# Partial sums of a down projection: kept in SBUF and added to DRAM at the end, with a larger descriptor store

## The chip, the cores and the metric

The kernel runs on one core of a Trainium2 chip. The metric is device time in microseconds (us), the median of several runs; one further run was profiled, and all rows of a trace come from that one. The engines of the core are named as in the profile: PE (matrix multiply), PEld (its weight loads), DVE (vector), ACT (activations and copies), POOL (general, and the one that issues DMAs through descriptors that it writes itself into a store in SBUF) and SP (issues most DMAs). Every engine works through its own queue in order and waits on semaphores of the others.

## The reference, cut to what matters

The reference is one inference step of a small encoder with two layers. Nine tiles of 128 tokens (1024 prompt tokens and 128 sample tokens) by 1024 features run through, in each layer, an attention with its output projection, and then a squared-ReLU MLP:

```python
def mlp(x, g_norm, w_up, w_down):
    return jnp.square(jax.nn.relu(rmsnorm(x, g_norm) @ w_up)) @ w_down
...
        hp = hp + ap @ w_o_a[i]
...
        hp = hp + mlp(hp, g_mlp[layer], w_up[layer], w_down[layer])
        hs = hs + mlp(hs, g_mlp[layer], w_up[layer], w_down[layer])
```

w_up is 1024 x 4096, w_down 4096 x 1024, everything is float32. The change touches the MLP and, a little, the output projection ahead of it.

## The kernel before, in words

**Number format.** Each float32 operand of a matmul is split into a high part (ACT, a cast) and the rest (DVE, a subtraction), helper `split`, lines 125 to 134. A product is three matmuls: high by high, high by low, low by high (`mm3`, lines 744 to 748).

**Stages.** A layer is attention (`attention`), output projection (`wo_phase`), up stage (`mlp_up`) and down stage (`mlp_down`), layer after layer (`run`, lines 1280 to 1301). The running sum x of the nine tiles lives in DRAM as `xp`, three parts of three tiles (`PARTS`: part 0 is tiles 5, 6, 7; part 1 is 2, 3, 4; part 2 is the sample tile, 0 and 1); `xd[t]` is tile t of it.

**Up stage** (lines 778 to 908). 16 blocks of 256 columns of w_up; products of sums of blocks, Strassen-like, in the PSUM tiles X, Y and Z. In each block `sample` multiplies the sample tile into `ps_s8`; ACT applies ReLU and square into an SBUF tile `h8` (128 x 256); `turn` (lines 838 to 843) transposes its two halves on PE (L841) and ACT copies them to the first 128 columns of the two h tiles `eh` (L843). The last three products of a block go to Y, X and Y; between the two in Y, DVE evicts Y (L878, `tt(v[3], Y, v[3])`). The h tiles and sums of them go to DRAM in 20 forms (`hd`), by POOL DMAs (L911).

**Down stage** (lines 968 to 1157). 40 steps (20 products for each half of the 4096 rows), in an order written out as `CHAINS`. A step n takes one form of h (`a`, 128 x 1536, loaded from `hd` by SP, L1026, split by ACT and DVE) and one sum of blocks of w_down (`r`, loaded by SP, L1026; sum `s` by DVE, L1062; split into `w`), and does 36 matmuls of 128 x 512 into three PSUM banks `ps_c`, one bank for each of three token tiles. Steps of one chain add up in the same banks; six banks allow two sets. `reads` of a step tells to which halves of which parts of x the banks are added after it. There are two ways:

- The part's x tiles are in SBUF already: DVE adds the bank to the tile (L1141).
- They are not: ACT copies the bank to one of two tiles `o` (L1138), and POOL adds the tile of three banks to `xp` in DRAM by an accumulating DMA of 768 KB (L1148). The two `o` tiles are used in turn, by steps 0, 1, 2, 3, 4, 8, 9, 10, 11, 12, 14, 28, 31 and 32.

`X_AT = {1: 2, 12: 1, 32: 0}` says that part 2 is loaded to SBUF after step 1, part 1 after step 12 and part 0 after step 32, each as three POOL DMAs from `xd` (`load_x`, L1084) that must wait for the accumulates into the same rows. After the last step that reads a part (30 for part 2, 35 for part 1, 39 for part 0) SP stores its three tiles (L1145): to `xd` in layer 0, to the output in layer 1.

**What sets the order.** A planner of the framework lays out each engine's queue from priorities and a simulation. The kernel adds orders by hand: `behind(a, b)` puts b after a on their engine, `follow` keeps PE's products, `chain` DVE's instructions of the down stage and `load` SP's loads in the order of the program. The loads of the first three steps and the splits of step 0 (`low[0]`: first that of `a`, then that of `w`) are emitted before the loop over the steps and have a raised priority, so that they run beside the last up block. `late` is a list of form sums of the last up blocks that DVE does in the first down steps. In layer 0, `prep_bias` (lines 1164 to 1194) and the next layer's first weight loads and splits (POOL L185, DVE L190) run beside the down stage.

**Memory.** POOL's DMAs take their descriptors from a store whose size is `dynamic_dma_scratch_size` (line 1849), 1024 bytes in each partition. The tiles of the down stage are laid out by `DOWN_HOME` over those of the up stage; a pad of 504 floats behind the bias tiles keeps the places of the rest.

**Output projection** (lines 643 to 735). `load_o` loads the attention's output of a tile from DRAM; in layer 1 it has two halves to be added, the second of which is loaded to a tile `o2`, and DVE adds them.

Of the kernel before, what the change touches and what calls it, by code (L numbers as in the profile page):

```python
# [8 lines left out]
F32 = mybir.dt.float32  # L9
F32R = mybir.dt.float32r  # L10
AF = mybir.ActivationFunctionType
ALU = mybir.AluOpType
# [4 lines left out]
P = 128  # L17
# [10 lines left out]
FB = 256  # L28
# [66 lines left out]
class Build:  # L95
# [547 lines left out]
    def wo_phase(self, layer, sx, x8, wo):  # L643
        nc = self.nc
        with ExitStack() as st:
            self.psum_pools(st, f"wo{layer}", dict(m=(4, 1), g=(3, 1)), dict(m="m", n="g"))
            work = self.pool(st, f"wow{layer}")
            small = self.pool(st, f"wosm{layer}", 2)
            osp, xs = {}, {}
            lo, hi = slice(0, 512), slice(512, 1024)  # L650

            def O(t, z):
                if t in self.kept:
                    xs[t] = self.kept[t]
                    return
                if len(xs) % 5 < 2:
                    xs[t] = self.rawp.tile([P, D], F32, tag="raw", name="x")
                else:
                    xs[t] = work.tile([P, D], F32, tag="x", name="x", bufs=3)
                nc.sync.dma_start(xs[t], self.xd[t])  # L660
                if t in self.wo_done:
                    return
                with self.tc.high_priority(WO_PRIO) if len(osp) < 2 else nullcontext():
                    load_o(t, z)

            def second():
                self.last = work.tile([P, 4, P], F32, tag="o2", name="o2")
                return self.last

            def load_o(t, z):  # L670
                o = work.tile([P, 4, P], F32, tag=f"o{z}", name="o")
                self.load_halves(layer, 1, t, o, second, nc.vector)
                oh = work.tile([P, 4, P], F32R, tag=f"oh{z}", name="oh")
                ol = work.tile([P, 4, P], F32R, tag=f"ol{z}", name="ol")
                self.split(oh, ol, o)
                osp[t] = oh, ol

            def M(t):
                x = xs[t]
                for n in range(2) if t not in self.wo_done else ():  # L680
# [36 lines left out]
            for n, t in enumerate(order):  # L717
                if n + 2 < NTILE:
                    O(order[n + 2], z % 2)
                    z += order[n + 2] not in self.wo_done  # L720
                M(t)
                ready.add(t)
                for f in pend:
                    f()
                pend = []
                if t == ST:
                    def sample():
                        for h in range(2):
# [49 lines left out]
    def mlp_up(self, layer, sx, x8, rp, raw0):  # L778
        nc = self.nc
        tt = nc.vector.tensor_tensor  # L780
        with ExitStack() as st:
# [36 lines left out]
            def act(t, src):  # L818
                a = nc.scalar.activation(t, src, AF.Relu)
                nc.scalar.activation(t, t, AF.Square)  # L820
                return a

            def sample(quad):
                s8 = self.psum("s", [P, FB], "ps_s8")
                z = []
                for h in range(2):
                    for k in range(4):
                        kk = h * 4 + k
                        z.append(self.mm3(
                            s8, x8[0][:, kk], x8[1][:, kk], quad[h][0][:, k], quad[h][1][:, k],  # L830
                            kk == 0, kk == KC - 1,
                        ))
                self.follow(z[0][0], z[-1][1])
                h8 = hp.tile([P, FB], F32, tag="h8", name="h8")
                self.marks = [act(h8, s8)]
                return h8

            def turn(eh, h8):
                t8 = self.psum("t", [P, 2, P], "ps_t8")
                for h in range(2):  # L840
                    nc.tensor.transpose(t8[:, h], h8[:, h * P : h * P + P], self.ident)  # L841
                for h in range(2):
                    nc.scalar.copy(eh[h][:, 0:P], t8[:, h])  # L843

            def tokens(eh, quad, ws, c, with_sample):
# [25 lines left out]
                product(X, 5, False, True)  # L871
                nc.scalar.copy(v[1], X)
                if with_sample:
                    h8 = sample(quad)
                product(X, 6, False, True)
                a = nc.scalar.copy(v[3], X)
                product(Y, 4, True, True)
# [4 lines left out]
                product(X, 3, False, True)  # L882
                act(v[2], X)
                if with_sample:
                    turn(eh, h8)
                product(Y, 2, False, True)
                tt(v[1], Y, v[1], ALU.add)
                act(v[1], v[1])
# [79 lines left out]
    def mlp_down(self, layer, out):  # L968
# [3 lines left out]
        with ExitStack() as st:  # L972
# [15 lines left out]
            for n, tags in enumerate(DOWN_HOME):  # L988
                pool = self.pool(st, f"d{n}_{layer}")
                for t in tags.split():  # L990
                    if t == "bias":
                        self.bias_tiles(pool)
                        pool.tile([P, 504], F32, tag="pad", name="pad")
                    elif t[0] == "+":
                        pool.tile([P, int(t[1:])], F32, tag="gap", name="gap")
                    else:
                        homes[t] = pool
                        slots[t] = fresh(t)
# [79 lines left out]
            def early(n):  # L1078
                return self.tc.high_priority(EARLY[n]) if n < len(EARLY) else nullcontext()

            def load_x(i):
                for t in PARTS[i]:
                    xs[t] = take(f"x{t}")
                    nc.gpsimd.dma_start(xs[t], self.xd[t])  # L1084

            for n in range(AHEAD):
                with early(n):
# [8 lines left out]
            def chain(z):  # L1096
# [2 lines left out]
                self.dve = z  # L1099
                return z  # L1100

            for z in (*low[0], total_of.get(1)):
                if z is not None:
                    chain(z)
            late = iter(self.late)
            for n, (s, p, g, first, final, reads, _) in enumerate(seq):
# [17 lines left out]
                for i in range(3):  # L1124
# [11 lines left out]
                    for o, v in reads:  # L1136
                        if o in adds:
                            nc.scalar.activation(adds[o][:, i], banks[i], AF.Copy, scale=float(v))  # L1138
                            continue
                        x = xs[PARTS[o // 2][i]][:, N[o % 2]]  # L1140
                        chain(tt(x, x, banks[i], ALU.add if v > 0 else ALU.subtract))  # L1141
                    for part in {o // 2 for o, _ in reads}:
                        if last[part] == n:
                            t = PARTS[part][i]
                            nc.sync.dma_start(out(t), xs[t])  # L1145
                for o, z in adds.items():
                    dst = self.xp[o // 2][:, :, N[o % 2]].rearrange("t p n -> p t n")
                    nc.gpsimd.dma_start(dst, z, accum_op=ALU.add)  # L1148
                if n in X_AT:
                    load_x(X_AT[n])  # L1150
                for _, z in zip(range(LATER), late):
                    chain(z)
                for m in range(n + 1, total):
# [657 lines left out]
TAIL = 6  # L1811
LATER = 3
AHEAD = 3
X_AT = {1: 2, 12: 1, 32: 0}
WO_ORDER = [[0, 4, 1, 5, 2, 6, 7, 3, ST], [0, 4, 1, 5, 6, 2, 7, 3, ST]]

CFG = [
# [49 lines left out]
```

## Time and profile before

| | us |
|---|---|
| median of 3 runs | 2400.55 (2395.85 to 2406.25) |
| profiled run, its own time | 2405.0 |
| its span, first to last instruction | 2403.2 |
| PE busy in the span | 2285.3 |
| DVE busy | 1735.2 |
| ACT busy | 1317.3 |
| POOL busy | 632.8 |

A row of a timeline gives the start in us, the duration in us, the engine, the line, the operation, what it writes and reads, the shape and the count; in brackets stands how long the engine had been idle before it, and what ended that. A row of the groups gives the count, then busy us and the mean of one in ns, then the idle time before the group's instructions and what ended most of it. A row of the waits gives the waiting engine and line, for what it waited, the total in us, how often, and the longest. A row of the windows gives busy time and, in parentheses, the count of each engine, then the granted PE clock, the busy share of the DMA engines and GB/s. A busy PE is not PE at its peak: its matmuls overlap, and 36 of 128 x 512 follow each other at a spacing well below the duration of one.

### The profile page before, as it was taken

How to read it: one execution, taken by the hardware profiler on the slowest of the kernel's cores; microseconds unless marked ns; L12 is line 12 of the kernel's file. 1: busy time of each engine (PE TensorE's matmuls, PEld its weight loads, DVE VectorE, ACT ScalarE, POOL GpSimd, SP SyncE). 2: the span in 40 equal slices, each digit the busy share in tenths (PEclk: the TensorE clock that was granted, in tenths of full speed). 3: DMA queues.
4: the chain of work that ended last, by engine and by line, in shares of the span. 5: the costliest groups of instructions: out<-in, count | busy, mean ns of one | idle time of the engine just before them, and what ended most of it. 6: DMA issues, size and time to landing. Idle time of an engine off the chain costs nothing.

```text
span 2403.2 us, 33331 instructions
## 1 busy us (share of the span) xinstructions
PE 2285.3 (95%) x11429; PEld 1904.2 (79%) x11429; DVE 1735.2 (72%) x3108; ACT 1317.3 (55%) x2587; POOL 632.8 (26%) x938
## 2 busy tenths in 40 slices
PE   7998999899999978999999999998999999889999
PEld 6787877788888767887777788886888888678887
DVE  6788786666566567998677876877665664678986
ACT  3777674555555534444367666665655555444452
POOL 4333332222222111002333434354122222111000
PEclk9999999999999989999999999999999999999999
DMA  7335546234343789657554655555243444878554
GB/s 251 120 111 166 170 149 200 88 131 147 125 139 124 222 241 228 209 145 232 190 153 113 194 154 176 166 171 168 86 147 122 143 147 138 255 169 227 193 155 148
DMA packets 227577, 397.41 MB, mean 165 GB/s; under 512 B 51592, under 2 KB 126288, under 8 KB 227408
## 3 DMA queue, kind: packets, MB, share of 16 engines
q1 hardware_dynamic: 190544, 291.45, 38.2%
q0 software_dynamic: 35568, 99.11, 14.5%
q10 hardware_dynamic: 1296, 4.72, 0.5%
q8 instruction: 90, 1.47, 0.3%
q14 instruction: 79, 0.65, 0.1%
HBM read 241.23 MB, written 152.92 MB: 164 GB/s over the span
## 4 chain that ended last, share of the span: by engine, by line
PE 76%; DVE 8%; DMA 7%; issue 4%; ACT 3%; POOL 1%; SPq 0%; ACTq 0%; POOLq 0%; DVEq 0%
PE ps_c L746 7%; PE ps_c L747 7%; PE ps_c L748 7%; PE ps_x L746 5%; PE ps_x L748 5%; PE ps_x L747 5%; PE ps_mm L217 4%; PE ps_mm L219 3%; PE ps_mm L218 3%; PE ps_y L746 2%; PE ps_y L748 2%; PE ps_y L747 2%; DMA a<-hd 2%; PE ps_tr L324 2%; PE ps_mm L176 1%
## 5 line engine op out<-in xcount | busy, mean ns | idle before, releaser
L746 PE MATMUL ps_c<-w,a 128*128 128x512 f32 x960 | 377.5, 393 | 36.0 <-ACT o L1138 27.8
L747 PE MATMUL ps_c<-w,a 128*128 128x512 f32 x960 | 376.3, 392 | 3.0 <-DVE w L134 3.0
L748 PE MATMUL ps_c<-w,a 128*128 128x512 f32 x960 | 375.7, 391 | 0.0
L911 POOL DMA_DIRECT2D hd<-h x272 | 149.0, 548 | 608.2 <-ACT h L820 368.8
L746 PEld LDWEIGHTS ps_c<-w,a 128*128 128x128 f32 x960 | 182.1, 190 | 76.2 <-ACT o L1138 29.0
L747 PEld LDWEIGHTS ps_c<-w,a 128*128 128x128 f32 x960 | 182.2, 190 | 41.8 <-DVE w L134 3.7
L748 PEld LDWEIGHTS ps_c<-w,a 128*128 128x128 f32 x960 | 181.8, 189 | 38.1
L128 ACT CAST a<-a 128x1536 fp32r<-128x1536 f32 x80 | 118.7, 1484 | 158.7 <-DMA a<-hd 158.7
L134 DVE TENSOR_TENSOR a<-a 128x1536 fp32r<-128x1536 f32 x80 | 140.3, 1753 | 78.0 <-ACT a L128 77.8
L217 PE MATMUL ps_mm<-w,hh 128*128 128x512 f32 x432 | 173.9, 404 | 7.6 <-POOL w L185 2.6
L219 PE MATMUL ps_mm<-w,hl 128*128 128x512 f32 x432 | 172.7, 401 | 1.0 <-DMA hl<-hTd 0.8
L218 PE MATMUL ps_mm<-w,hh 128*128 128x512 f32 x432 | 171.8, 399 | 1.3 <-DVE w L190 1.1
L746 PE MATMUL ps_x<-sx,w 128*128 128x512 f32 (+1 forms) x408 | 158.3, 388 | 3.9 <-ACT h L867 2.7
L128 ACT CAST w<-s 128x2048 fp32r<-128x2048 f32 x56 | 107.0, 1912 | 95.7 <-DVE s L1062 90.8
L1148 POOL DMA_DIRECT2D xp<-o x28 | 36.3, 1297 | 464.2 <-ACT o L1138 364.6
L128 ACT CAST w<-ru 128x512 fp32r<-128x512 f32 (+1 forms) x160 | 110.0, 708 | 84.1 <-PE ps_y L747 32.0
L748 PE MATMUL ps_x<-sx,w 128*128 128x512 f32 (+1 forms) x408 | 154.7, 379 | 0.0
L747 PE MATMUL ps_x<-sx,w 128*128 128x512 f32 (+1 forms) x408 | 154.7, 379 | 0.0
L134 DVE TENSOR_TENSOR w<-s,w 128x2048 fp32r<-128x2048 f32 x56 | 128.2, 2289 | 30.7 <-ACT w L128 30.7
L134 DVE TENSOR_TENSOR ptl<-ps_tr,pth 128x512 fp32r<-128x512 f32 x180 | 122.3, 685 | 24.3 <-ACT pth L128 19.2
L134 DVE TENSOR_TENSOR w<-ru,w 128x512 fp32r<-128x512 f32 (+1 forms) x160 | 126.7, 794 | 14.9 <-ACT w L128 14.8
L128 ACT CAST pth<-ps_tr 128x512 fp32r<-128x512 f32 x180 | 105.0, 595 | 45.7 <-PE ps_tr L324 37.2
(269 smaller groups left out, 6098.2 us busy)
## 6 DMA issues: line engine op xcount, KB each, us to landing
a<-hd SPq DMA_DIRECT2D x80, 768.0 KB, 4.8
hd<-h POOLq DMA_DIRECT2D x272, 192.0 KB, 2.5
ru<-in_w_up SPq DMA_DIRECT2D x64, 512.0 KB, 3.8
r<-in_w_down SPq DMA_DIRECT2D x32, 1024.0 KB, 9.4
xp<-o POOLq DMA_DIRECT2D x28, 768.0 KB, 7.7
o<-oTd SPq DMA_DIRECT2D x52, 256.0 KB, 4.5
x<-xp SPq DMA_DIRECT2D x23, 512.0 KB, 4.9
xp<-xo SPq DMA_DIRECT2D x18, 512.0 KB, 2.8
```

Source lines behind the costliest of these rows:

```text
L128: a = nc.scalar.copy(hi, src)
L134: return a, e.tensor_tensor(lo, src, hi.bitcast(F32), ALU.subtract)
L176: nc.tensor.matmul(ps, oh[:, k, :], w[:, 0, k, nn], start=(k == 0), stop=False)
L217: nc.tensor.matmul(ps, a, w[:, 0, k, :], start=(k == 0), stop=False)
L218: nc.tensor.matmul(ps, a, w[:, 1, k, :], start=False, stop=False)
L219: self.lp = nc.tensor.matmul(ps, b, w[:, 0, k, :], start=False, stop=(k == KC - 1))
L324: self.lp = nc.tensor.transpose(pt[:, i, :], get(i), self.ident)
L746: a = mm(ps, ah, bh, start=first, stop=False, skip_group_check=True)
L747: mm(ps, ah, bl, start=False, stop=False, skip_group_check=True)
L748: return a, mm(ps, al, bh, start=False, stop=last, skip_group_check=True)
L911: return lambda p, z: self.nc.gpsimd.dma_start(self.hd[c // 4][:, p, c % 4], z)
L1148: nc.gpsimd.dma_start(dst, z, accum_op=ALU.add)
```

## The change

- **Parts 2 and 1 of x** are no longer loaded. Their tiles start empty (`fresh_x`); the first bank for each tile and half is copied into the tile by ACT, the later ones are added by DVE as before. After the part's last step POOL adds the tile to `xd` by an accumulating DMA of 512 KB, where SP stored it before. In layer 1 a POOL DMA copies it from `xd` to the output, three steps later in the program. The accumulates by way of `o` (the steps listed above) stay as they are.
- **Part 0** (`HELD`) is loaded after step 34 and not 32, by SP in its order of loads and not by POOL; it is stored by SP as before.
- **The descriptor store** grows from 1024 to 2048 bytes.
- **The last Y eviction of the up stage** (L878 of the last block) is put ahead of the first weight split of the down stage on DVE.
- **Room** for the larger store: `h8` goes; the sample's ReLU and square are done in two halves straight into `eh`, transposed from there and copied back. `o2` goes; the second half is loaded to the tile that later takes the high part. The pad of 504 floats becomes 248.

```diff
             def load_o(t, z):
                 o = work.tile([P, 4, P], F32, tag=f"o{z}", name="o")
-                self.load_halves(layer, 1, t, o, second, nc.vector)
                 oh = work.tile([P, 4, P], F32R, tag=f"oh{z}", name="oh")
                 ol = work.tile([P, 4, P], F32R, tag=f"ol{z}", name="ol")
+                self.last = oh.bitcast(F32)
+                self.load_halves(layer, 1, t, o, lambda: self.last, nc.vector)
                 self.split(oh, ol, o)
...
                 self.follow(z[0][0], z[-1][1])
-                h8 = hp.tile([P, FB], F32, tag="h8", name="h8")
-                self.marks = [act(h8, s8)]
-                return h8
-
-            def turn(eh, h8):
+                self.marks = []
+                for h in range(2):
+                    self.marks.append(act(eh[h][:, 0:P], s8[:, h * P : h * P + P]))
+
+            def turn(eh):
                 t8 = self.psum("t", [P, 2, P], "ps_t8")
                 for h in range(2):
-                    nc.tensor.transpose(t8[:, h], h8[:, h * P : h * P + P], self.ident)
+                    nc.tensor.transpose(t8[:, h], eh[h][:, 0:P], self.ident)
...
-                        pool.tile([P, 504], F32, tag="pad", name="pad")
+                        pool.tile([P, 248], F32, tag="pad", name="pad")
...
-            def load_x(i):
+            fresh_x = set()
+
+            def start_x(i):
                 for t in PARTS[i]:
                     xs[t] = take(f"x{t}")
-                    nc.gpsimd.dma_start(xs[t], self.xd[t])
+                    if i == HELD:
+                        load(xs[t], self.xd[t])
+                    else:
+                        fresh_x.update((t, h) for h in range(2))
+
+            def store_x(i, t):
+                if i == HELD:
+                    nc.sync.dma_start(out(t), xs[t])
+                    return
+                nc.gpsimd.dma_start(self.xd[t], xs[t], accum_op=ALU.add)
+                if out(t) is not self.xd[t]:
+                    copies.append((n + 3, t))
+
+            copies = []
...
+            self.behind(self.marks[-1], low[0][1])
             for z in (*low[0], total_of.get(1)):
...
-                        x = xs[PARTS[o // 2][i]][:, N[o % 2]]
+                        t = PARTS[o // 2][i]
+                        x = xs[t][:, N[o % 2]]
+                        if (t, o % 2) in fresh_x:
+                            fresh_x.remove((t, o % 2))
+                            nc.scalar.activation(x, banks[i], AF.Copy, scale=float(v))
+                            continue
                         chain(tt(x, x, banks[i], ALU.add if v > 0 else ALU.subtract))
                     for part in {o // 2 for o, _ in reads}:
                         if last[part] == n:
-                            t = PARTS[part][i]
-                            nc.sync.dma_start(out(t), xs[t])
+                            store_x(part, PARTS[part][i])
...
                 if n in X_AT:
-                    load_x(X_AT[n])
+                    start_x(X_AT[n])
+                for m, t in copies:
+                    if m == n:
+                        nc.gpsimd.dma_start(out(t), self.xd[t])
...
-X_AT = {1: 2, 12: 1, 32: 0}
+X_AT = {1: 2, 12: 1, 34: 0}
+HELD = 0
...
-    nc = bacc.Bacc("TRN2", target_bir_lowering=False, num_devices=1, dynamic_dma_scratch_size=1024)
+    nc = bacc.Bacc("TRN2", target_bir_lowering=False, num_devices=1, dynamic_dma_scratch_size=2048)
```

More of the change, by code (lines that the diff above doesn't have):

```diff
@@ L664, in O @@
                     load_o(t, z)
-            def second():
-                self.last = work.tile([P, 4, P], F32, tag="o2", name="o2")
-                return self.last
             def load_o(t, z):
                 o = work.tile([P, 4, P], F32, tag=f"o{z}", name="o")
-                self.load_halves(layer, 1, t, o, second, nc.vector)
                 oh = work.tile([P, 4, P], F32R, tag=f"oh{z}", name="oh")
                 ol = work.tile([P, 4, P], F32R, tag=f"ol{z}", name="ol")
+                self.last = oh.bitcast(F32)
+                self.load_halves(layer, 1, t, o, lambda: self.last, nc.vector)
                 self.split(oh, ol, o)
@@ L821, in act, with sample @@
                 return a
-            def sample(quad):
+            def sample(eh, quad):
                 s8 = self.psum("s", [P, FB], "ps_s8")
@@ L873, in tokens @@
                 if with_sample:
-                    h8 = sample(quad)
+                    sample(eh, quad)
                 product(X, 6, False, True)
@@ L884, in tokens @@
                 if with_sample:
-                    turn(eh, h8)
+                    turn(eh)
                 product(Y, 2, False, True)
```

## The prediction

> **What bounds the kernel now.** The page's chain of what ended last comes first: PE holds three quarters of it, so the time is matmul time plus PE's idle time. Among the page's costliest groups, the first matmul of the down stage is the one with idle time worth having, and most of that ended on ACT's eviction into o (L1138).
>
> ```profile
> PE 76%; DVE 8%; DMA 7%; issue 4%; ACT 3%; POOL 1%; SPq 0%; ACTq 0%; POOLq 0%; DVEq 0%
> ...
> L746 PE MATMUL ps_c<-w,a 128*128 128x512 f32 x960 | 377.5, 393 | 36.0 <-ACT o L1138 27.8
> ```
>
> The waits, longest first, say what ACT itself waited for (the landing of an earlier accumulate from the same o buffer), and that POOL's accumulates stood 56.9 us waiting for nothing visible ("issue").
>
> ```profile
> POOL xp L1148 <- issue: 56.9, 8, 11.9
> ACT o L1138 <- DMA xp<-o: 50.0, 9, 17.5
> ```
>
> PE's timeline gives the places: before step 5 of the down stage, in both layers. I count steps from 0; one is 36 matmuls.
>
> ```profile
> 864.82 0.79 PE L746 MATMUL ps_c<-w,a 128*128 128x512 f32 x1 [13.79 <-ACT o L1138]
> ...
> 874.61 0.39 PE L746 MATMUL ps_c<-w,a 128*128 128x512 f32 x1
> ...
> 882.77 0.39 PE L746 MATMUL ps_c<-w,a 128*128 128x512 f32 x1
> ...
> 2109.14 0.79 PE L746 MATMUL ps_c<-w,a 128*128 128x512 f32 x1 [12.51 <-ACT o L1138]
> ...
> 2119.64 0.39 PE L746 MATMUL ps_c<-w,a 128*128 128x512 f32 x1
> ```
>
> The rows are the first matmuls of steps 5, 6 and 7 of layer 0 and of steps 5 and 6 of layer 1; the bracket is PE's idle time and what ended it. Step 6 takes 882.77 - 874.61 = 8.16 us, or 0.227 a matmul. Step 5, after the gap, takes 9.79 (layer 0) and 10.50 (layer 1): PE runs slow for a moment, another 1.63 and 2.34.
>
> Why did o not come free? ACT's timeline: the evictions of steps 2, 3 and 4 each begin when an earlier accumulate lands. POOL's timeline: the accumulates of steps 0, 1 and 2 and the x loads.
>
> ```profile
> 832.59 0.60 ACT L1138 ACTIVATE o<-ps_c 128x512 f32<-128x512 f32 x1 [3.60 <-DMA xp<-o]
> ...
> 834.82 1.08 ACT L1138 ACTIVATE o<-ps_c 128x512 f32<-128x512 f32 x2
> ...
> 841.57 0.60 ACT L1138 ACTIVATE o<-ps_c 128x512 f32<-128x512 f32 x1 [3.87 <-DMA xp<-o]
> ...
> 864.17 1.08 ACT L1138 ACTIVATE o<-ps_c 128x512 f32<-128x512 f32 x2 [17.49 <-DMA xp<-o]
> ```
>
> ```profile
> 819.56 1.38 POOL L1148 DMA_DIRECT2D xp<-o  x1 [5.21 <-ACT o L1138]
> 832.84 1.28 POOL L1148 DMA_DIRECT2D xp<-o  x1 [11.90 <-issue]
> ...
> 842.66 1.60 POOL L1084 DMA_DIRECT2D x<-xp  x3 [0.32 <-issue]
> ...
> 855.26 1.31 POOL L1148 DMA_DIRECT2D xp<-o  x1 [9.92 <-issue]
> ```
>
> The second accumulate goes out at 832.84, 0.25 after the first landed (832.59), though the two touch different buffers: the descriptor store takes one accumulate at a time. The third goes out at 855.26, behind three x loads, though step 2's last eviction ended at 834.82 + 1.08 = 835.9. It lands at 864.17, after 8.9. Step 4's evictions write the same o buffer, step 5's matmuls write the same PSUM banks as step 4's, and so PE stood until 864.82.
>
> The second place, in both layers too, is the last product of the up stage. PE's timeline around it, then DVE's of layer 0:
>
> ```profile
> 801.30 0.39 PE L748 MATMUL ps_x<-sx,w 128*128 128x512 f32 x1
> 805.61 0.50 PE L746 MATMUL ps_y<-sx,w 128*128 128x512 f32 x1 [3.92 <-DVE h L878]
> ...
> 810.05 0.40 PE L746 MATMUL ps_c<-w,a 128*128 128x512 f32 x1
> ...
> 2050.15 0.79 PE L746 MATMUL ps_y<-sx,w 128*128 128x512 f32 x1 [3.60 <-DVE h L878]
> ...
> 2055.44 0.59 PE L746 MATMUL ps_c<-w,a 128*128 128x512 f32 x1
> ```
>
> ```profile
> 798.17 1.76 DVE L134 TENSOR_TENSOR a<-a 128x1536 fp32r<-128x1536 f32 x1 [10.21 <-ACT a L128]
> 800.46 2.29 DVE L134 TENSOR_TENSOR w<-r,w 128x2048 fp32r<-128x2048 f32 x1 [0.53 <-ACT w L128]
> 802.67 2.29 DVE L1062 TENSOR_TENSOR s<-r,r 128x2048 f32<-128x2048 f32 x1
> 804.87 0.68 DVE L878 TENSOR_TENSOR h<-ps_y,h 128x512 f32<-128x512 f32 x1
> ```
>
> DVE, which works in order, does the down stage's first weight split (800.46) and a weight sum (802.67) ahead of the up stage's eviction L878, and the last Y product waits for the Y bank that L878 reads. Twelve matmuls of 0.227 are 2.72, but from 805.61 to 810.05 they took 4.44 and in layer 1 5.29: slow matmuls again.
>
> **The change, part by part.** *Descriptor store and x loads.* With twice the store a second accumulate goes out as soon as its evictions are done, and the loads of parts 2 and 1 are gone. Starting from the new time of step 0 (below): step 0's accumulate at 819.56 - 5.8 = 813.8; it lands after the 13.0 it took (819.56 to 832.59), step 1's and step 2's 8.7 behind each other (832.84 to 841.57): 844.2. Step 5 is due at 804.25 + 5 x 8.16 = 845.05. So the gap goes, with 0.85 us for an eviction of 0.6: just enough. Gain 13.79 + 1.63 + 12.51 + 2.34 = **30.3 us**. What is late next is the same wait, by a hair. Ends: nothing gained, or all of it; I take all, as this arithmetic gives.
>
> The slow matmuls behind the four gaps (1.63, 2.34 and, below, 1.72, 2.57) go with them. [...]
>
> *Last eviction ahead of the split.* The X product before ends at 801.53 and took 2.72, so Y is complete near 798.8. The a split ends at 799.93; L878 then runs to 800.6, before PE asks at 801.53. The w split moves from 800.46 to 800.6, ends at 802.9, and PE reaches step 0 at 801.53 + 2.72 = 804.25: 1.4 us of cover. Behind L878 wait, on DVE, that split and the sum for step 1; who waits for them is PE at step 0 and ACT's cast for step 1, wanted a whole step later. Gain 3.92 + 1.72 and 3.60 + 2.57 = **11.8 us**. From start to start each of the four gaps is 0.16 longer than its bracket says (805.61 - 801.53 = 4.08, not 3.92), since a matmul's modelled end lies behind the start of the next: **0.6 us** more, and step 0 comes 810.05 - 804.25 = 5.8 earlier.
>
> *First copies by ACT.* Per layer 12 adds (three tiles, two halves, two parts; steps 5, 6, 15, 19) become copies:
>
> ```profile
> L1141 DVE TENSOR_TENSOR x<-x,ps_c 128x512 f32<-128x512 f32 x162 | 104.4, 681 | 25.2 <-PE ps_c L748 22.8 <-ACT o L1138 2.2
> ...
> L1138 ACT ACTIVATE o<-ps_c 128x512 f32<-128x512 f32 x84 | 49.3, 596 | 85.5 <-DMA xp<-o 50.0 <-PE ps_c L748 35.4
> ...
> L843 ACT COPY h<-ps_t 128x128 f32<-128x128 f32 x64 | 13.7, 266 | 0.3
> ```
>
> DVE loses 8.2 us a layer, ACT gains 7.2. A bank is wanted again two banks (5.4 us) after it is done, so both hide: 0. Queued behind a copy on ACT are the casts of the next step. Without that cover a copy costs its 0.6, twelve of them 7 a layer.
>
> *Sample in the up stage.* Two ACT instructions of 128x256 (0.42 by the square below) become four of 128x128; by L843 some 4 x 0.27 = 1.06. ACT +0.2 to +0.4, in 32 blocks. ACT and then PE in one such block:
>
> ```profile
> 771.00 0.42 ACT L820 ACTIVATE h<-h 128x256 f32<-128x256 f32 x1
> ...
> 775.80 0.62 ACT L128 CAST w<-ru 128x512 fp32r<-128x512 f32 x1 [0.84 <-DVE ru L809]
> ```
>
> ```profile
> 775.86 0.38 PE L841 MATMUL ps_t<-identr,h 128*128 128x128 f32 x2
> ```
>
> The square ends at 771.42, the transposes come at 775.86: 4.4 us hide it. 0.
>
> *Ends of the parts.* Six SP stores a layer become accumulates on POOL behind DVE's last adds of steps 30 and 35; queued behind them on POOL are the accumulates of steps 31 and 32 and the next layer's weight splits (L185), and DVE waits for those. Layer 1 adds six copies, issued after steps 33 and 38. No row shows a copy between DRAM tensors; the nearest, the accumulate, reads and writes DRAM too and takes 7.7. One accumulate and three copies behind each other are 31, and step 35 leaves four steps, 32.6 us: hidden, by little; without cover the last copy's 7.7 shows at the end. At layer 0's boundary SP is rid of its stores ahead of the next layer's loads, while the weight splits may come later. I take 0 for all, and keep -5 (the 3.14 gap before step 36 below, with its slow matmuls) to +10 (the 9.54 that POOL waited there for a weight load).
>
> ```profile
> xp<-o POOLq DMA_DIRECT2D x28, 768.0 KB, 7.7
> ...
> 1112.93 1.68 POOL L1084 DMA_DIRECT2D x<-xp  x3 [7.02 <-DMA xp<-o]
> 1124.15 3.58 POOL L185 TENSOR_SCALAR w<-raw,gcol 128x512 fp32r<-128x512 f32 x4 [9.54 <-DMA raw<-in_w_kv]
> ```
>
> Part 0's loads move to SP after step 34. They wait there for the same landing (1112.9); behind them the activation load of step 37 is due seven us later: 0.
>
> *Second half of o* (output projection): layer 1, two tiles; the buffer is the tile's own: 0 either way.
>
> **Sum:** 30.3 + 11.8 + 0.6 = 42.7 us from the profiled 2405.0 (span 2403.2, 1.8 around it). The median of the runs is 2400.55, so 2400.55 - 42.7 = **2357.8**.
>
> **Rivals.** (1) *The DMA engines are the limit.* Just before the gap they had no idle time left:
>
> ```profile
> 835.00:851.00 16.00, 16.00 (x71) 12.95 (x69) 13.66 (x9) 7.56 (x8) 3.25 (x6) 1.00 1.02 322
> ```
>
> The column before the last is their share, 1.02. If every accumulate takes the first one's 13.0, step 2's lands at 813.8 + 39 = 852.8, 7.8 after step 5 is due; with 1.7 for slow matmuls that is 9.5 a layer, 19 in all: 2376.8. For it: that share. Against: three x loads of 512 KB were in it, and are gone. [...]
>
> (2) *The store is not what held POOL.* Then the x loads' absence alone lets step 2's accumulate go at 842.66; with 8.9 it lands at 851.6, 0.6 after the 851.0 at which step 5 was due (864.82 - 13.79). By two form stores that may go ahead, up to 4: 2 x 2.3 = 4.6, 2362.4.
>
> (3) *More goes.* Three gaps of layer 0 stand on late DVE or ACT work that the edit makes lighter:
>
> ```profile
> 912.27 0.66 PE L746 MATMUL ps_c<-w,a 128*128 128x512 f32 x1 [4.86 <-DVE x L1141]
> 926.46 0.50 PE L746 MATMUL ps_c<-w,a 128*128 128x512 f32 x1 [1.46 <-ACT o L1138]
> 1131.21 0.76 PE L746 MATMUL ps_c<-w,a 128*128 128x512 f32 x1 [3.14 <-DVE x L1141]
> ```
>
> Together 9.5: 2348.3. Against: the loads that they wait for are not in the diff.
>
> (4) *POOL's order at layer 0's end* puts the new accumulates ahead of the weight splits: +10, 2367.8.
>
> (5) *Slower.* In each up block ACT's two new instructions fall between its weight casts. PE does its work in order as well, so once the second half's square ends after 775.86 the transposes hold the next product. It decides at 4.4 us of delay; behind the cast that begins at 775.80 it would be some 1.7 late: 32 x 1.7 = 54, 2411.8.
>
> **How the numbers follow.** Forecast 0.57 (own range 2352 to 2366), (1) 0.16, (2) 0.06, (3) 0.10, (4) 0.06, (5) 0.05. The range reaches from (3), less a little, to (1): 2346 to 2380. Half a per cent (12 us) is what a measurement tells apart: below 2388.5 lie all but (5) and a tail of (1): faster 0.91, same 0.04, slower 0.05.
>
> **What would show it.** No PE gap before step 5 and none before the last Y product; step 5 at 8.16; accumulates of steps 0 and 1 both under way before the first lands; no "issue" wait on POOL; 138 adds at the x line. Wrong: a gap on o of over 4 us in step 5, PE waiting for the sample's transposes, or DVE late in step 0.

## The result and the profile after

| | before | after |
|---|---|---|
| median, us | 2402.62 (2395.85 to 2406.25, 4 runs) | 2368.5 (2365.73 to 2373.72, 4 runs) |
| profiled run, its own time | 2405.0 | 2373.72 |
| its span | 2403.2 | 2371.9 |

The ratio is 0.9864 (95% interval 0.9834 to 0.9894): 34 us faster, where 42.7 were forecast. 2368.5 lies within the range of the text (2346 to 2380), but 2.5 above the range that it gave to its forecast alone (2352 to 2366). The two profiled runs stand 31.3 apart.

PE's timeline of the kernel after, at the places shown of before: the last product of the up stage, then the first matmuls of steps 0, 5 and 6 of layer 0 and of steps 0 and 5 of layer 1.

```profile
801.77 0.39 PE L743 MATMUL ps_y<-sx,w 128*128 128x512 f32 x1
...
804.49 0.39 PE L743 MATMUL ps_c<-w,a 128*128 128x512 f32 x1
...
845.82 0.50 PE L743 MATMUL ps_c<-w,a 128*128 128x512 f32 x1
...
854.13 0.39 PE L743 MATMUL ps_c<-w,a 128*128 128x512 f32 x1
...
2032.37 0.39 PE L743 MATMUL ps_c<-w,a 128*128 128x512 f32 x1
...
2074.07 0.50 PE L743 MATMUL ps_c<-w,a 128*128 128x512 f32 x1 [0.28 <-ACT o L1151]
```

Of PE's waits shown of before, those of 3.92 and 13.79 us are gone, and that of 12.51 has become 0.28. Step 0 starts at 804.49 (before 810.05), step 5 takes 854.13 - 845.82 = 8.31.

POOL's accumulates of steps 0 to 2, and ACT's evictions that waited for them:

```profile
814.31 1.37 POOL L1165 DMA_DIRECT2D xp<-o  x1 [2.90 <-ACT o L1151]
822.60 1.27 POOL L1165 DMA_DIRECT2D xp<-o  x1 [6.92 <-ACT o L1151]
...
832.69 1.33 POOL L1165 DMA_DIRECT2D xp<-o  x1 [3.82 <-issue]
```

```profile
827.34 0.60 ACT L1151 ACTIVATE o<-ps_c 128x512 f32<-128x512 f32 x1 [3.37 <-DMA xp<-o]
...
845.17 0.60 ACT L1151 ACTIVATE o<-ps_c 128x512 f32<-128x512 f32 x1 [4.73 <-DMA xp<-o]
```

Step 1's accumulate goes out at 822.60, 4.7 before step 0's lands (827.34): two are under way. Step 2's lands at 845.17 (forecast 844.2), and PE starts step 5 at 845.82, as soon as that eviction is done. In the waits, POOL's 56.9 us of "issue" and ACT's 50.0 have become:

```profile
ACT o L1151 <- DMA xp<-o: 17.7, 5, 4.9
...
POOL xp L1165 <- issue: 3.8, 1, 3.8
```

What is new shows in the page's groups (the first row is of before, the others of after): the second matmul of a product had 3.0 us of idle time behind DVE's splits, and now has 8.6. The first matmul's 36.0 us have fallen to 8.8: the stall on `o` left, and another grew.

```profile
L747 PE MATMUL ps_c<-w,a 128*128 128x512 f32 x960 | 376.3, 392 | 3.0 <-DVE w L134 3.0
...
L743 PE MATMUL ps_c<-w,a 128*128 128x512 f32 x960 | 377.1, 393 | 8.8 <-DVE x L1159 5.7
L744 PE MATMUL ps_c<-w,a 128*128 128x512 f32 x960 | 376.6, 392 | 8.6 <-DVE w L134 8.6
```

### The profile page after: what moved, and what is told of

Read it like the earlier page. It is cut to its first block, busy times and chain, and to the rows that moved or that the text cites. A ratio compares the mean times of both kernels' runs of the same rounds, so it can differ in the third digit from the quotient of the medians.

```text
span 2371.9 us, 33381 instructions
## 1 busy us (share of the span) xinstructions
PE 2284.4 (96%) x11429; PEld 1903.3 (80%) x11429; DVE 1723.7 (73%) x3084; ACT 1326.7 (56%) x2675; POOL 626.0 (26%) x938
## 4 chain that ended last, share of the span: by engine, by line
PE 72%; DVE 9%; DMA 8%; ACT 4%; issue 4%; POOL 2%; SPq 0%; ACTq 0%; POOLq 0%; DVEq 0%
PE ps_c L743 6%; PE ps_c L744 6%; PE ps_c L745 6%; PE ps_x L743 5%; PE ps_x L745 5%; PE ps_x L744 5%; PE ps_mm L217 3%; PE ps_mm L219 3%; PE ps_mm L218 3%; DMA a<-hd 3%; PE ps_y L745 2%; PE ps_y L743 2%; PE ps_y L744 2%; PE ps_tr L324 2%; DVE w L134 2%
## 5 line engine op out<-in xcount | busy, mean ns | idle before, releaser
L908 POOL DMA_DIRECT2D hd<-h x272 | 148.8, 550 | 595.7 <-ACT h L817 373.5
L744 PEld LDWEIGHTS ps_c<-w,a 128*128 128x128 f32 x960 | 181.7, 189 | 48.2 <-DVE w L134 10.7
L134 DVE TENSOR_TENSOR w<-ru,w 128x512 fp32r<-128x512 f32 (+1 forms) x160 | 126.6, 793 | 14.7 <-ACT w L128 14.6
L816 ACT ACTIVATE h<-h 128x512 f32<-128x512 f32 (+1 forms) x102 | 61.9, 607 | 123.3 <-DVE h L866 93.3
```

The costliest lines, as they stand in the source:

```text
L134: return a, e.tensor_tensor(lo, src, hi.bitcast(F32), ALU.subtract)
L744: mm(ps, ah, bl, start=False, stop=False, skip_group_check=True)
L908: return lambda p, z: self.nc.gpsimd.dma_start(self.hd[c // 4][:, p, c % 4], z)
```

## The experiments

A step's length is from its first matmul to the next step's (step 39: to its last matmul's end). The table gives, from one profile of each kernel, how far groups of steps exceed 8.16 us a step, "up" the time from the last block's transposes to step 0 (both layers), and the median with the ratio's interval. Label e9 is the changed kernel again.

| kernel | 4, 5 both layers | up | 21 to 23 both | 35 to 39 layer 0 | 39 layer 1 | median | ratio to before |
|---|---|---|---|---|---|---|---|
| before | 30.6 | 24.0 | 0.0 | 7.6 | 1.6 | 2402.62 | |
| after | 0.9 | 11.4 | 3.1 | 9.1 | 4.8 | 2368.5 | 0.9834 to 0.9894 |
| e9 | 0.1 | 11.9 | 2.4 | 10.2 | 5.7 | 2369.47 | 0.9843 to 0.9881 |
| e1 | 29.7 | 11.5 | 0.0 | 6.4 | 1.6 | 2386.6 | 0.992 to 0.9966 |
| e2 | 13.6 | 20.8 | 0.0 | 7.0 | 1.8 | 2377.63 | 0.9881 to 0.9925 |
| e3 | 23.2 | 11.4 | 1.9 | 12.6 | 6.6 | 2392.88 | 0.9936 to 0.9975 |
| e4 | 0.4 | 22.8 | 1.7 | 9.0 | 5.0 | 2378.32 | 0.9883 to 0.9932 |
| e5 | 1.3 | 11.5 | 0.0 | 12.3 | 6.6 | 2364.26 | 0.9825 to 0.987 |
| e6 | 0.5 | 11.7 | 2.8 | 11.6 | 2.1 | 2367.8 | 0.9833 to 0.9875 |
| e7 | 0.8 | 11.6 | 0.0 | 8.1 | 1.8 | 2358.72 | 0.9796 to 0.9842 |
| e8 | 12.0 | 11.6 | 0.0 | 5.9 | 1.8 | 2372.11 | 0.9851 to 0.9897 |
| e10 | 0.9 | 11.4 | 0.0 | 7.2 | 1.8 | 2362.38 | 0.9804 to 0.985 |

Two stretches hold the attention and the output projection: from the start to the first up product of layer 0, and from the last down product of layer 0 to the first up product of layer 1. Together they take 941.0 us before, 939.5 and 937.0 in the two profiles of the changed kernel, and 932.2 to 939.5 in the others. So a few us between any two times lie where no run shows an edit to act. The two down stages together take 701.4 before, and 681.2 and 680.5 after.

Theory: the forecast's two terms came as forecast, and part 1's partial sums cost the missing part. Rivals: one of the terms fell short; or the store, the sample's new form or part 0's late load cost it.

### e1: the order alone

The kernel before, with the line

```diff
+            self.behind(self.marks[-1], low[0][1])
```

> The kernel before with one line added: the last Y eviction of the up stage stands ahead of the first weight split on DVE. Theory (the order and the accumulates are separate costs): step 0 starts 5.5 us earlier in each layer, the accumulates of steps 0 to 2 move forward with it, the gaps before step 5 stay at 13.8 and 12.5 us, and the time falls by 11 us. Rival (the accumulates stand on something that does not move, such as the form stores of the up stage or a full set of DMA engines): the gaps before step 5 grow by up to 5.5 us each and the time falls by 0 to 3.

"Up" falls by 12.5, and steps 4 and 5 keep their 30: the accumulates moved forward together with step 0. The theory holds. The median fell by 17; the interval (-8 to -19) holds 11, and the profile shows nothing else at a place that this line touches (4 us of the rest lie in the attention and output projection).

### e2: the store alone

```diff
-    nc = bacc.Bacc("TRN2", target_bir_lowering=False, num_devices=1, dynamic_dma_scratch_size=1024)
+    nc = bacc.Bacc("TRN2", target_bir_lowering=False, num_devices=1, dynamic_dma_scratch_size=2048)
```

(with the room for it: h8, o2 and the pad as in the change)

> The kernel before with the 2048-byte store and the edits that make room for it (no h8, no o2, smaller pad), nothing else; the x loads stay. Theory (store and x loads hold POOL one after the other, so that one alone brings part): the accumulate of step 1 goes out before that of step 0 lands, but the three x loads still wait for landings in the same rows and hold step 2's accumulate behind them; the gaps shrink to 5 to 9 us each, and the time falls by 8 to 16 us. Rival (the store is the whole cause): the gaps go, -25 to -30. Rival (the store is not what held POOL): the accumulates go out as before, 0. A fourth reading, that twice the DMAs in flight and the sample's new form cost time, gives a rise.

The time fell by 26 us, more than expected, but of that only 30.6 - 13.6 = 17.0 lie in steps 4 and 5, just above the theory's upper end of 16, and 3.0 at the last product of layer 1. The other 6 of the profile lie in the attention and the output projection. The edit touches one place there, a buffer in the output projection of layer 1; from its first product to the first up product that takes 30.6 us before and 27.8 here, but also 28.4 in e1, which keeps the buffer. So these 6 can't be put down to the edit. "The whole cause" falls: gaps of 4.39 and 3.63 us stay. POOL and then ACT and PE in layer 0:

```profile
823.46 1.28 POOL L1145 DMA_DIRECT2D xp<-o  x1 [6.66 <-ACT o L1135]
...
833.33 1.61 POOL L1081 DMA_DIRECT2D x<-xp  x3 [4.70 <-DMA xp<-o]
...
836.02 1.35 POOL L1145 DMA_DIRECT2D xp<-o  x1
```

```profile
850.62 1.08 ACT L1135 ACTIVATE o<-ps_c 128x512 f32<-128x512 f32 x2 [9.23 <-DMA xp<-o]
```

```profile
851.27 0.79 PE L743 MATMUL ps_c<-w,a 128*128 128x512 f32 x1 [4.39 <-ACT o L1135]
```

Step 1's accumulate (823.46) no longer waits for the landing of step 0's (827.25). Step 2's still stands behind the x loads, goes out 2.7 us after them (836.02 - 833.33), and takes 850.62 - 836.02 = 14.6 us to land, where it took 845.17 - 832.69 = 12.5 after the change.

### e3: the partial sums alone

The changed kernel with these two lines as before:

```diff
-            self.behind(self.marks[-1], low[0][1])
...
-    nc = bacc.Bacc("TRN2", target_bir_lowering=False, num_devices=1, dynamic_dma_scratch_size=2048)
+    nc = bacc.Bacc("TRN2", target_bir_lowering=False, num_devices=1, dynamic_dma_scratch_size=1024)
```

> The changed kernel with the store back at 1024 bytes and without the line that orders the last Y eviction; the partial sums in SBUF, the first copies by ACT and part 0's loads on SP stay. Theory (store admits one accumulate at a time): the accumulate of step 1 still waits for the landing of step 0's, step 2's then goes at once and lands some 9 us behind it; the gaps before step 5 shrink from 13.8 and 12.5 us to 1 to 3 us, and the time falls by 20 to 27 us. Rival (the store is the larger part): gaps of 6 us and more stay, and the time falls by 10 to 15. If the gaps are gone altogether, the store brought nothing here.

The theory as sized here falls, and the rival's sizes come: 11 us, gaps of 6.21 and 12.47 us, and steps 4 and 5 give only 7.4 of 30.6, nearly all of it in layer 0. (Here the planner put the eviction ahead of the split by itself, "up" 11.4; what this brings is lost again in the last three groups of steps of the table, 11.9 us.) POOL and PE in layer 1:

```profile
2049.47 1.34 POOL L1164 DMA_DIRECT2D xp<-o  x1 [4.48 <-issue]
2063.23 1.28 POOL L1164 DMA_DIRECT2D xp<-o  x1 [12.42 <-issue]
2064.04 1.06 POOL L908 DMA_DIRECT2D hd<-h  x1
2075.63 1.63 POOL L908 DMA_DIRECT2D hd<-h  x3 [10.53 <-issue]
...
2081.11 1.32 POOL L1164 DMA_DIRECT2D xp<-o  x1 [3.85 <-ACT w L128]
```

```profile
2092.71 0.80 PE L743 MATMUL ps_c<-w,a 128*128 128x512 f32 x1 [12.47 <-ACT o L1150]
```

Without a single x load, the gap of layer 1 is as long as before (in layer 0 it is 6.21, where it was 13.79). With the small store the accumulates alternate with the form stores of the last up blocks (L908), and these stand in "issue" as well: 62.3 us here (28 times, up to 10.5), 4.0 in the changed kernel (18 times, up to 0.4). Step 2's goes out 2081.11 - 2075.63 = 5.5 us behind three of them that had stood for 10.53. The forecast and the expectation had counted the accumulates alone.

### e4: all but the order

```diff
-            self.behind(self.marks[-1], low[0][1])
```

> The changed kernel without the line that orders the last Y eviction. Theory (the parts add up): 11 us slower than the changed kernel, which is some 23 us faster than the kernel before; gaps of 3.9 and 3.6 us before the last Y product, none before step 5. Rival (later start of step 0 gives the accumulates more or less room): the difference to the changed kernel is below 6 or above 16 us.

10 us slower than the changed kernel (2378.32 against 2368.5), with 11.4 of it at "up". The order adds up with the rest.

### e5: the first copies on DVE

```diff
-                            nc.scalar.activation(x, banks[i], AF.Copy, scale=float(v))
+                            chain(nc.vector.tensor_scalar(x, banks[i], float(v), None, ALU.mult))
```

> The changed kernel with the twelve first copies of a layer on DVE, in its chain, and not on ACT. Theory (at step 19 the copies stand on ACT behind a cast that waits for its load, and DVE's adds behind the copies): steps 21 to 23 return to 8.16 us, 1.4 us less in layer 0 and 1.8 in layer 1, the time falls by 3 us. Rival (DVE has no room either, or the late load is the cause by itself): steps 21 to 23 stay long, 0, or grow by some 0.6 us per copy.

In the changed kernel, ACT, then DVE, then PE from step 19 on:

```profile
971.62 0.60 ACT L1157 ACTIVATE x<-ps_c 128x512 f32<-128x512 f32 x1 [0.76 <-PE ps_c L745]
976.30 1.48 ACT L128 CAST a<-a 128x1536 fp32r<-128x1536 f32 x1 [4.08 <-DMA a<-hd]
977.68 1.08 ACT L1157 ACTIVATE x<-ps_c 128x512 f32<-128x512 f32 x2
```

```profile
973.11 0.68 DVE L1159 TENSOR_TENSOR x<-x,ps_c 128x512 f32<-128x512 f32 x1
978.31 0.69 DVE L1159 TENSOR_TENSOR x<-x,ps_c 128x512 f32<-128x512 f32 x1 [4.53 <-ACT x L1157]
```

```profile
985.72 0.50 PE L744 MATMUL ps_c<-w,a 128*128 128x512 f32 x1 [0.31 <-DVE w L134]
```

The second and third copy stand on ACT behind a cast that waits for its load; DVE's chained add waits for the copy, and its splits are late for PE. With the copies on DVE, the cast waits for its load just as long, and nothing behind it does:

```profile
972.46 1.48 ACT L128 CAST a<-a 128x1536 fp32r<-128x1536 f32 x1 [4.44 <-DMA a<-hd]
```

```profile
970.26 0.68 DVE L1157 TENSOR_SCALAR x<-ps_c 128x512 f32<-128x512 f32 x1
970.86 0.68 DVE L1159 TENSOR_TENSOR x<-x,ps_c 128x512 f32<-128x512 f32 x1
```

Steps 21 to 23 are at 8.16 in both layers, so that the copies' place on ACT is shown as the cause there. The time is 4 to 5 us below the changed kernel's two medians, with overlapping intervals, and is not shown to come from this: in the profile the two groups of steps at the ends are longer than in either profile of the changed kernel (12.3 and 6.6 us over), and the two down stages take 683.0, about 2 us more. What steps 21 to 23 gain is lost again there; why stays open.

### e6: part 1's copies by SP, behind the last activation load

```diff
                 for m, t in copies:
-                    if m == n:
+                    if m == n and m < total - 2:
                         nc.gpsimd.dma_start(out(t), self.xd[t])
...
+            for m, t in copies:
+                if m >= total - 2:
+                    load(out(t), self.xd[t])
```

> The changed kernel with the copies of part 1 to the output (layer 1, three of 512 KB) issued by SP behind the activation load of step 39, and not by POOL after step 38. Theory (the copies that move on the DMA engines with that load make it late): the load takes 4 to 4.5 us, not 5.5, step 39 of layer 1 falls from 12.9 to 10 us, the time by 3 us, and the copies stay hidden before the end. Rival (the accumulates of part 1, not the copies, hold the load up): step 39 stays at 12 us or more, 0. Rival (the copies now end last): up to 8 us more.

The changed kernel at the end of layer 1: POOL's copies, SP's load of the activations of step 39, ACT's cast of them, PE.

```profile
2334.93 0.54 POOL L1170 DMA_DIRECT2D out<-xp  x1 [3.87 <-DMA xp<-x]
...
2340.50 0.53 POOL L1170 DMA_DIRECT2D out<-xp  x1 [4.13 <-DMA xp<-x]
2344.20 0.51 POOL L1170 DMA_DIRECT2D out<-xp  x1 [3.17 <-DMA xp<-x]
```

```profile
2346.61 0.32 SPq L1023 DMA_DIRECT2D a<-hd  x1
```

```profile
2352.12 1.48 ACT L128 CAST a<-a 128x1536 fp32r<-128x1536 f32 x1 [2.98 <-DMA a<-hd]
```

```profile
2357.65 0.50 PE L744 MATMUL ps_c<-w,a 128*128 128x512 f32 x1 [2.69 <-DVE w L134]
```

The same load in e6, with the copies behind it:

```profile
2344.42 0.32 SPq L1023 DMA_DIRECT2D a<-hd  x1
2344.86 2.12 SPq L1023 DMA_DIRECT2D out<-xp  x3
```

```profile
2348.85 1.48 ACT L128 CAST a<-a 128x1536 fp32r<-128x1536 f32 x1 [1.55 <-DMA a<-hd]
```

From issue to cast 4.4 us, not 5.5, and step 39 falls from 12.9 to 10.2: the copies were the cause. PE's wait there falls from 2.69 to 1.60 us; the rest is the granted clock behind it, 0.57 from 2359 to 2363 in the changed kernel and 1.00 from 2355 to 2359 in e6. In the changed kernel the last copy, issued at 2344.20, landed after 3.8 us, 1.4 us into the load; in e6 the copies go out 0.44 us behind the load in SP's own queue. By what way they lengthen the load in the one case and not in the other is not shown. The median fell by 0.7 us only, so that the gain is shown at step 39 and not in the time; in the profiled execution steps 35 to 39 of layer 0, which the edit does not touch, took 2.4 longer than in the changed kernel's first profile.

### e7: only part 2 as partial sums

```diff
-                    if i == HELD:
+                    if i == 0:
                         load(xs[t], self.xd[t])
+                    elif i in HELD:
+                        nc.gpsimd.dma_start(xs[t], self.xd[t])
...
-                if i == HELD:
+                if i in HELD:
                     nc.sync.dma_start(out(t), xs[t])
...
-HELD = 0
+HELD = 0, 1
```

> The changed kernel with only part 2 kept as partial sums; part 1 is loaded by POOL after step 12 and stored by SP after step 35, as in the kernel before. Theory (what the change lost, it lost to part 1: steps 21 to 23, the end of layer 0, step 39 of layer 1): these steps return to the kernel before's times, steps 4 and 5 stay at 8.2 to 8.6, and the time is 6 to 9 us below the changed kernel, near 2360. Rival (the losses come from the larger store or from the late load of part 0): within 2 us of the changed kernel.

2358.72 us, 10 below the changed kernel and the fastest of all. In the profile the two down stages take 674.4, 6 to 7 less than in the changed kernel's two; the attention and output projection have the lowest value of all, 932.2, so that the rest may be luck. Steps 4 and 5 keep the whole gain, steps 21 to 23 are back at 8.16, step 39 of layer 1 at 10.0, the end of layer 0 at 8.1 over. The page's groups:

```profile
L743 PE MATMUL ps_c<-w,a 128*128 128x512 f32 x960 | 376.3, 392 | 8.3 <-DVE x L1161 4.9
L744 PE MATMUL ps_c<-w,a 128*128 128x512 f32 x960 | 375.6, 391 | 5.5 <-DVE w L134 5.5
```

The part that cost the time is the one whose load was never in the way: only part 2's loads stand ahead of step 2's accumulate.

### e8: store and order, no partial sums

The kernel of e2 with the line of e1.

> The kernel before with the larger store (and its room) and the order of the last Y eviction, but no partial sums. Theory (the store by itself brought 26 us, the order 12 us, and they add up): 38 us faster than the kernel before, 2365, which is 2 to 4 us faster than the changed kernel, so that the partial sums as made bring nothing in all; the gaps before step 5 are 3.5 to 5 us. Rival (with step 0 earlier, the accumulates meet more of the form stores): gaps of 6 us or more, and a time 3 us or more above the changed kernel's.

2372.11, 29 faster than before and some 3 us above the changed kernel's two medians, with overlapping intervals. The expected 2365 was 7 too low, since it took the 26 us of e2 whole, where 6 could not be put down to the edit. The gaps before step 5 are 3.95 and 4.21 us, as the theory says, and steps 4 and 5 keep 12.0, near e2's 13.6. So the partial sums gain 11 to 12 there and lose 9 to 11 in the last three groups of steps: of all that they save in steps 4 and 5, little is left.

### e9 and e10

> The changed kernel once more, beside the next kernel on one chip. Expected 2365 to 2371 as before; what its steps show twice is the kernel's (steps 21 to 23 long, the stall before step 37 of layer 0, step 39 of layer 1 at 12 to 13 us, none before step 5), and what they show once is one execution's (step 7 of layer 1 at 9.3, the slow first block of the up stage).

2369.47. The same steps are long as in the first profile (step 39 of layer 1 with 13.8 us a little beyond what was expected), and step 7 of layer 1 (9.31 then) is at 8.16: that was one execution's.

```diff
-                    if i == 0:
-                        load(xs[t], self.xd[t])
-                    elif i in HELD:
+                    if i in HELD:
                         nc.gpsimd.dma_start(xs[t], self.xd[t])
...
-X_AT = {1: 2, 12: 1, 34: 0}
+X_AT = {1: 2, 12: 1, 32: 0}
```

(against e7)

> The kernel with only part 2 kept as partial sums, and part 0 loaded by POOL after step 32 as in the kernel before, not by SP after step 34. Theory (part 0's loads on SP, ahead of the next layer's weight loads, set the stall before step 37 of layer 0): steps 35 to 39 of layer 0 fall from 48.9 to some 47 us, and the time by 2 us against the kernel with part 2 alone. Rival (the stall is the next layer's weight splits' own and only moves to another step): the sum of these five steps stays within 1 us, and so does the time within 2.

The five steps sum to 0.9 less than in e7, as the rival says; the median is 3.7 higher, where the rival allowed 2, with overlapping runs (2355.79 to 2366.66 against 2355.89 to 2360.22). Where part 0 is loaded decides nothing that can be measured here. This is a second kernel with part 2 alone as partial sums, and its down stages take 673.9: against the changed kernel it is 6 to 7 us faster, by the medians and in the down stages.

## Why the prediction was right, and what it missed

The profiled times stand 31.3 apart, 42.7 were forecast: 11.4 short. By its steps:

- **Descriptor store and x loads, 30.3 us: right.** Steps 4 and 5 lost 29.7. The landing at 844.2 that decides it was measured at 845.17, "by a hair" as forecast, and steps 4 and 5 kept 0.9. What the term left together, the experiments take apart: the store alone gives 17.0, the sums with the small store 7.4, both 29.7. Each removes one of two things that held step 2's accumulate, and the sums need the store, since with the small one the form stores stand in "issue" too (62.3 us in e3). Step 0's accumulate took 13.0 (827.34 - 814.31), as forecast, and from its landing to step 2's there are 845.17 - 827.34 = 17.8, where 2 x 8.7 = 17.4 were forecast. That this sum fits is luck, since its two parts do not: step 1's accumulate landed 9.7 us after its issue at 822.60, so near 832.3 and 5 behind step 0's, and step 2's came 13 behind that. Nor did step 2's go out as soon as its last eviction was done (830.36 + 1.08 = 831.4): it went out at 832.69, 0.4 after step 1's had landed and behind 3.82 us of "issue", so that the larger store, as it seems, held it up as well, for 1.3 us.
- **Last eviction, 11.8 + 0.6 us: right.** 12.6 at "up" with the rest, and 12.5 alone (e1).
- **First copies by ACT, 0: the step that failed.** The text asked when the bank is wanted again (5.4 us) and what stands behind the copy on ACT. It did not ask what stands ahead of the copy, a cast that waits for a load, nor who waits for the copy: DVE's next add and the splits chained behind it (4.08 us of ACT's wait, 4.53 of DVE's). 3.1 us in the two layers, gone when the copies are on DVE (e5).
- **Ends of the parts, 0 within -5 to +10: mis-sized.** The copies did end under the last steps, as worked out, yet the last of them was still under way when the last activation load began, which took 5.5 us to the cast and 4.4 with the copies behind it: 3.2 us at step 39 of layer 1 (e6). At layer 0's end 1.5 us more in the profile and 2.6 in e9; the stall of 3.14 before step 36 became one of 3.13 before step 37. In the table the six profiles with part 1's sums (after, e3 to e6, e9) have 9.0 or more there, and those without 8.1 or less. The traces show where part 1's accumulates may do this. PE waits there for a split that stands on DVE behind a weight split of the next layer, that one waits for POOL (L185), and POOL for a load by SP (L146). From that load's issue to POOL's start there are 6.3 us (after, the first four rows), with the accumulates (L1092) under way, and 3.9 before (the last two); 6.3 to 7.0 in the six profiles with part 1's sums, 3.8 to 3.9 in the other six. From 1109.86 to 1116.19 (after) POOL's queue takes 55.8% of the 16 DMA engines' time and SP's, with three loads in it, 35.4%; from 1127.20 to 1131.08 (before) SP's takes 48.2% and POOL's nothing. So it looks like step 39 once more, a load that is waited for beside POOL's transfers; no run moves these accumulates alone.

```profile
1109.24 0.87 POOL L1092 DMA_DIRECT2D xp<-x  x1
...
1109.86 0.37 SPq L146 DMA_DIRECT2D raw<-in_w_kv  x1
...
1116.19 1.35 POOL L185 TENSOR_SCALAR w<-raw,gcol 128x512 fp32r<-128x512 f32 x2 [3.23 <-DMA raw<-in_w_kv]
...
1121.00 0.80 PE L744 MATMUL ps_c<-w,a 128*128 128x512 f32 x1 [3.13 <-DVE w L134]
```

```profile
1127.20 0.37 SPq L146 DMA_DIRECT2D raw<-in_w_kv  x1
...
1131.08 1.21 POOL L185 TENSOR_SCALAR w<-raw,gcol 128x512 fp32r<-128x512 f32 x1 [3.35 <-DMA raw<-in_w_kv]
```

- **Sample, part 0 by SP, second half of o, 0:** right as far as can be measured; no stall of PE on the sample's transposes came.
- The rest: steps 0 and 1, 0.5; step 7 of layer 1, 1.2, once; the first up block of each layer, 1.5 each, of which more below; other stretches -1.5.

The rivals: (1), the DMA engines: the slow accumulates that it counts on came in e2, where the x loads stay (14.6 us for one), and in part in the changed kernel: the DMA share from 820 to 846 is 1.07, and the three accumulates take 13.0, 9.7 and 12.5 us, near the rival's 13.0. But they overlap, and step 2's lands at 845.17, not at 852.8. That the rival's 2376.8 stands 8 us from the result and the forecast's 2357.8 stands 11 has other reasons. The 1.7 us that its sum takes for slow matmuls is the author's estimate, and no run shows it as the one figure for a gap: the rows of before show 1.63 to 2.57 (granted clock 0.85 from 865 to 875, in step 5 of layer 0, and 0.77 from 2109 to 2119.5, in that of layer 1), and e2 shows 2.3 and 3.0. (2), the store did not hold POOL, falls with e2. (3) did not come: steps 9 to 11 of layer 0 are 8.5 over in both kernels. (4): 1.5 to 2.6 us came at layer 0's end and not 10, and not by POOL's order: ahead of that split POOL stood idle for 3.23 us until the load was there. (5) did not come. Of the signs listed, the "issue" wait did not vanish (3.8 us, once) and step 5 is at 8.31 and 8.29, not 8.16; the others came.

## What to carry to other kernels

When a change takes several things out of one stall, ask of each part whether the stall needs it: here only the part whose loads stood ahead of the accumulate paid, and the other cost 6 to 11 us by the medians, 6 to 7 in the down stages. An instruction moved to an engine with room inherits the waits that stand ahead of it there, and passes them to whoever is chained behind it (here 4.08 us on ACT, then 4.53 on DVE). A transfer that is hidden itself may still delay a small late load that is not; put it behind that load in the same queue (5.5 us from the load's issue to the cast became 4.4 so, in e6).

## What the runs showed of the hardware

In the first up block of layer 0, where PE is busy for only 3.1 to 3.7 of each 5 us from 435 to 450, its granted clock fell to 0.77 and then 0.55 in the changed kernel and stayed at 1.00 in e1, though its longest wait there is the same, 1.36 and 1.35 us (the changed kernel, then e1):

```profile
447.34 0.39 PE L743 MATMUL ps_x<-sx,w 128*128 128x256 f32 x1 [1.36 <-ACT h L864]
```

```profile
446.95 0.39 PE L746 MATMUL ps_x<-sx,w 128*128 128x256 f32 x1 [1.35 <-ACT h L867]
```

The windows around and behind it, in the same order (the column before the last two is the granted clock):

```profile
445.00:450.00 5.00, 3.62 (x20) 2.91 (x18) 5.00 (x9) 3.12 (x6) 0.00 (x0) 0.77 0.47 119
450.00:455.00 5.00, 4.50 (x22) 4.50 (x23) 0.34 (x1) 1.48 (x4) 0.00 (x0) 0.55 0.27 93
```

```profile
445.00:450.00 5.00, 3.13 (x24) 2.69 (x24) 4.95 (x8) 4.02 (x8) 0.00 (x0) 1.00 0.48 130
450.00:455.00 5.00, 5.00 (x44) 5.00 (x43) 0.42 (x1) 2.01 (x5) 0.00 (x0) 1.00 0.22 77
```

The stretch from the first up product to the first transposes takes 35.17 us in the one and 32.44 in the other, 2.7 us more with the lower clock. In the twelve profiles it takes 32.4 to 32.6 in seven, 33.7 in two and 35.2 in three, and the changed kernel itself has both 35.2 and 33.7 (e9): one of the things by which runs of the same kernel differ. Behind the gaps of 4.39 and 3.63 us in e2, step 5 took 2.3 and 3.0 us too long.
